# One load for both heads' block of the inverses of the delta-rule scans, issued with the group's features, and two pools opened in the other order

## The chip, the cores and the metric

The kernel runs on one core of a Trainium2 chip, as one launch. The metric is the device time of that launch in microseconds (us). The core has TensorE (PE; PEld is its weight load), VectorE (DVE), ScalarE (ACT), GpSimd (POOL) and SyncE (SP), which here issues the transfers (DMAs).

## The reference

The reference is a trunk of two layers on 256 latent and 256 context tokens of width 2048, in float32. Layer 0 is a bidirectional RWKV-7 mixer with 32 heads of 64, layer 1 is a retention with 8 heads; each stands between an RMSNorm with adaLN and a gated residual add. The change lies in layer 0. Its core, cut to what matters, is this recurrence for each direction and head:

```python
def step(S, inp):
    r_t, w_t, k_t, v_t, kk_t, a_t = inp
    sa = jnp.einsum('bhvk,bhk->bhv', S, kk_t)
    S = S * w_t[:, :, None, :] - sa[..., None] * (kk_t * a_t)[:, :, None, :] + v_t[..., None] * k_t[:, :, None, :]
    return S, jnp.einsum('bhvk,bhk->bhv', S, r_t)
S_c, oc = wkv7_scan(S0, r_c, w_c[d], k_c[d], v_c, kk_c, a_c[d], d == 1)
_, ol = wkv7_scan(S_c, r_l, w_l[d], k_l[d], v_l, kk_l, a_l[d], d == 1)
```

The outputs of both directions are added, normed by head, gated with silu(g) and multiplied by `w_out`.

## The kernel before

**Stages.** Layer 0 runs through `layer0_proj` (the big projections), `layer0_k` (features of the scans from L658 on) and `scans` (L1205); then comes layer 1. The recurrence is not run token by token. Tokens are cut into chunks of 64; inside a chunk the delta rule is a triangular system. Its matrix is inverted by blocks of 32, and the chunk then takes a few matrix products.

**Names.** `layer0_k` writes the features of 16 tiles (two heads each) to `fD` in DRAM, and the 32x32 blocks to invert to `Ld`. `inverse` (L1100) runs for a pair of tiles E on POOL: it loads 128 blocks into invX (L1108), makes 30 steps of a multiply and an add (L1116, L1123), sets the diagonal (L1127), stores the inverses to `Td` (L1131), and after a transposed copy on DVE (L1133) half of them to `T1d` (L1134).

**The scans** take pairs of tiles E = 0, 2, ..., 14, each in four groups q. For a group, `loads` brings the features of both tiles into two of four ft buffers: 512 columns each (L1225, 512 KB; a chunk's matrices), 384 (L1232) and 128 (L1233), and four uv transfers (L1230). `tloads` brings the inverses: at q = 0 two t1 loads (L1261), and for every group eight loads of 32 partitions x 4 x 32 numbers (L1267, 16 KB) into one of two tt buffers, one for each chunk half, block and head. An ft buffer is free again when the products of `outs` (L1420, L1427) have read it, a tt buffer when L1358 has.

In `ahead`, `first` (L1298; needs the ft of 512 columns and t1), ACT's copy L1305, `second` (L1311; needs tt) and ACT's copy L1319 make the blocks' corner in tt; L1286 makes zv. A `step` then takes L1339 (state by features), z on DVE (L1344), L1358 (with tt), uv on ACT (L1364), L1371 and the new state on DVE (L1384). Between these stand the products of the output matrix (`out_chunk`, L1552), whose weights are loaded at L1535 and split into two parts, whi on ACT (L1542) and wlo on POOL (L1543); their other operand yx is split likewise (L1523, L1524). `gpass` stores the gate's part ge to `gT` (L796).

**What sets the order.** Every piece of work is given to a wheel with a time, `W.at(time, function, job, needs, frees)`. The wheel sorts the pieces by time, holds one back while a ring of buffers that it needs is full (and whatever belongs to the same job with it), and writes their instructions in that order; for PE, DVE, ACT and POOL it pins the order (L123, L150). SP's queue is not pinned: there the scheduler of the framework puts the transfers in order by its own timeline. SP issues in order, and a transfer that waits holds those behind it. `open_scans2` (L1182) opens the pools of the scans' second half, in the memory that earlier pools left; the place of a pool decides whose release its first users wait for.

## Time and profile before

| what | value |
|---|---|
| runs: median, lowest, highest of 3 | 2752.47, 2752.12, 2758.63 us |
| profiled execution, its own time | 2755.28 us |
| its span | 2753.5 us |
| busy PE, DVE, ACT, POOL | 2633.9, 1518.4, 1311.2, 746.4 us |
| the scans | about 1000 to 1680 us of the span |
| tt loads (L1267) | 256, of 16 KB, landing 2.3 us after issue (median) |
| ft loads of 512 columns (L1225) | 64, of 512 KB, landing 6.1 us after issue (median) |

One execution is taken by the profiler; starts count from the beginning of its span. In a timeline row stand start, length, engine, line, operation, out<-in, and in brackets the idle time before and what ended it. In a row by window stand the window, its length, the busy time of PE, PEld, DVE, ACT and POOL with their instructions, the granted clock of TensorE (1.00 is full), the share of time in which the 16 DMA engines were busy, and GB/s. SPq is SP's queue, where a row's length is that of the issue, not of the transfer.

### The profile page before, as it was taken

What the parts mean: (1) busy time and instruction counts of PE and PEld (TensorE: products, weight loads), DVE (VectorE), ACT (ScalarE), POOL (GpSimd) and SP (SyncE); (2) the same over time, 40 slices, a digit from 0 to 9 for tenths busy, and PEclk for the clock granted to TensorE, in tenths of its full rate; (3) what the DMA queues carried; (4) which work ended last, traced back from release to release, by engine and by line L of the source; (5) the groups of instructions that cost most, each with busy time, mean ns of one, the idle gap of its engine ahead of it and who ended that gap; (6) DMA issues with size and microseconds to landing.
All of it is one profiled execution on the core that took longest, in us unless ns stands there. A gap on an engine that the chain in (4) does not pass through costs nothing. (4 is left out here: it accounts for less than half of the span.)

```text
span 2753.5 us, 48167 instructions
## 1 busy us (share of the span) xinstructions
PE 2633.9 (96%) x18572; PEld 2137.5 (78%) x18580; DVE 1518.4 (55%) x2629; ACT 1311.2 (48%) x2212; POOL 746.4 (27%) x843
## 2 busy tenths in 40 slices
PE   6999999999998999988999998999999999999998
PEld 5576578777776778867778785888888888899886
DVE  3565853668888822344444456955555644434444
ACT  5243742567777634544444444544445433334443
POOL 0002400000004765665666532300000099600000
PEclk9999999999999999998999999999999999999999
DMA  9868884469899787776767665655555766545654
GB/s 335 311 245 309 287 286 127 138 196 276 259 267 270 226 240 199 198 232 200 213 192 203 165 193 192 227 205 176 171 173 180 257 221 225 196 138 159 202 192 159
DMA packets 543095, 594.70 MB, mean 216 GB/s; under 512 B 118017, under 2 KB 375953, under 8 KB 540049
## 3 DMA queue, kind: packets, MB, share of 16 engines
q1 hardware_dynamic: 542866, 591.62, 68.2%
q8 instruction: 147, 2.41, 0.4%
q14 instruction: 82, 0.67, 0.1%
HBM read 464.11 MB, written 127.40 MB: 215 GB/s over the span
## 5 line engine op out<-in xcount | busy, mean ns | idle before, releaser
L400 DVE TENSOR_TENSOR wlo<-wraw,whi 128x1024 fp32r<-128x1024 f32 (+1 forms) x368 | 462.8, 1259 | 563.3 <-ACT whi L399 557.5
L399 ACT CAST whi<-wraw 128x1024 fp32r<-128x1024 f32 (+1 forms) x368 | 375.4, 1024 | 603.0 <-PE ps_acc L426 177.0
L426 PE MATMUL ps_acc<-whi,xop 128*128 128x512 f32 x1024 | 305.3, 393 | 1.3 <-DVE ev L648 0.8
L1926 PE MATMUL ps_acc<-xop,whi 128*128 128x256 f32 (+1 forms) x1024 | 253.9, 340 | 1.3 <-ACT xop L1677 1.1
L426 PEld LDWEIGHTS ps_acc<-whi,xop 128*128 128x128 f32 x1024 | 192.3, 189 | 45.3 <-issue 2.9
L1552 PE MATMUL ps_b<-yx,whi 128*128 128x512 f32 x512 | 206.9, 441 | 7.6 <-ACT yx L1523 6.4
L1926 PEld LDWEIGHTS ps_acc<-xop,whi 128*128 128x128 f32 x1024 | 176.7, 191 | 24.2 <-ACT xop L1677 1.4
L1826 PEld LDWEIGHTS ps_b<-ax,xop 128*128 128x128 f32 x1536 | 190.8, 188 | 4.9 <-DVE ah L400 0.3
L1826 PE MATMUL ps_b<-ax,xop 128*128 128x256 f32 x1536 | 194.4, 282 | 0.1
L426 PE MATMUL ps_acc<-wlo,xop 128*128 128x512 f32 x512 | 186.7, 392 | 0.0
L1899 POOL TENSOR_TENSOR wga<-wga,cst 128x512 f32<-128x512 f32 x64 | 69.3, 1103 | 415.6 <-DMA wga<-in_ada_w 415.6
L1364 ACT ACTIVATE uv<-ps_p 64x128 f32<-64x128 f32 x256 | 69.7, 272 | 230.4 <-PE ps_p L1358 217.0
L732 PE MATMUL ps_acc<-xop,whi 128*128 128x512 f32 x512 | 177.0, 405 | 2.0 <-DVE ev L648 2.0
L583 PE MATMUL ps_acc<-xop,whi 128*128 128x512 f32 x512 | 161.6, 401 | 14.3 <-ACT xop L399 13.2
L1926 PE MATMUL ps_acc<-xop,wlo 128*128 128x256 f32 (+1 forms) x512 | 171.8, 338 | 1.1 <-DVE wlo L400 1.1
L1384 DVE SCALAR_TENSOR_TENSOR s<-ps_p,ec,qs 64x64 f32<-64x64 f32 x384 | 108.5, 283 | 100.7 <-PE ps_p L1371 89.9
L1876 PE MATMUL ps_acc<-whi,ah 128*128 128x512 f32 x512 | 161.5, 395 | 1.9 <-DVE ah L400 1.9
L426 PE MATMUL ps_c<-whi,xop 128*128 128x512 f32 x512 | 155.4, 390 | 0.0
L1123 POOL TENSOR_TENSOR invX<-invX,invT 128x30 f32<-128x30 f32 (+14 forms) x240 | 134.3, 560 | 15.7
L583 PEld LDWEIGHTS ps_acc<-xop,whi 128*128 128x128 f32 x512 | 95.9, 191 | 53.4 <-ACT xop L399 16.8
L1543 POOL TENSOR_TENSOR wlo<-wraw,whi 128x512 fp32r<-128x512 f32 (+1 forms) x48 | 79.5, 1656 | 203.8 <-ACT whi L1542 186.4
L1116 POOL TENSOR_TENSOR invT<-invX 128x30 f32<-128x30 f32 (+14 forms) x240 | 125.2, 521 | 16.4 <-DMA invX<-Ld 1.1
(300 smaller groups left out, 5588.5 us busy)
## 6 DMA issues: line engine op xcount, KB each, us to landing
wada<-in_ada_w SPq DMA_DIRECT2D x72, 1024.0 KB, 8.5
wraw<-in_rt_w_in SPq DMA_DIRECT2D x64, 1024.0 KB, 5.2
wraw<-in_rk_w_in SPq DMA_DIRECT2D x72, 512.0 KB, 4.8
fD<-it SPq DMA_DIRECT2D x64, 512.0 KB, 4.2
ft<-fD SPq DMA_DIRECT2D x64, 512.0 KB, 6.1
wraw<-in_rt_w_in SPq DMA_DIRECT2D x64, 512.0 KB, 4.6
wraw<-in_rt_w_out SPq DMA_DIRECT2D x32, 1024.0 KB, 5.1
wraw<-in_rk_w_in SPq DMA_DIRECT2D x28, 1024.0 KB, 5.9
```

The costliest lines, as they stand in the source:

```text
L399: self.nc.scalar.copy(hi, src)
L400: (eng or self.nc.vector).tensor_tensor(lo, src, hi.bitcast(F32), ALU.subtract)
L426: nc.tensor.matmul(pt, xop(d)[:, x_, xs], ws[k // 2][w_][:, k % 2, sl], start=(d == 0 and n == 0), stop=(d == nk - 1 and n == 2))
L583: nc.tensor.matmul(acc[i], (hi, lo)[w_][:, kk, 128 * i:128 * i + 128], xs[ds[k]][:, x_, :], start=(k == 0 and n == 0), stop=(k == nk - 1 a ...
L732: nc.tensor.matmul(st["acc"][i], st["s", d // 4][w_][:, d % 4, 128 * i:128 * i + 128], self.kx[d][:, x_, :], start=(d == 0 and m == 0), st ...
L1116: nc.gpsimd.tensor_tensor(tmp[:, 0:j, 0:n], X[:, 0:j, j].unsqueeze(2).broadcast_to([128, j, n]), X[:, j, j + 1:].unsqueeze(1).broadcast_to ...
L1123: nc.gpsimd.tensor_tensor(X[:, 0:j, j + 1:], X[:, 0:j, j + 1:], tmp[:, 0:j, 0:31 - j], ALU.add)
L1384: nc.vector.scalar_tensor_tensor(dst, src, ec, R["qs", d][H, H], ALU.mult, ALU.add)
L1552: nc.tensor.matmul(Q["p", i], Q["s", i // 2][w_][:, k, 128 * (i % 2):128 * (i % 2) + 128], st["yx", e0 + k][:, x_, :], start=(k == 0 and r ...
L1826: nc.tensor.matmul(pt[:, TL * j:TL * j + TL], ht[e][:, w_, 128 * k:128 * k + 128], ax[:, k, x_, :], start=(k == 0 and n == 0), stop=(k == ...
L1876: nc.tensor.matmul(acc[m], y[:, x_, kk, 128 * m:128 * m + 128], ws[w_][:, kk, :], start=(p == 0 and kk == 0 and n == 0), stop=(p == 7 and ...
L1926: nc.tensor.matmul(acc[i][:, 0:nt], w_[:, kk, 128 * i:128 * i + 128], x[:, x_, 0:nt], start=(d == 0 and n == 0), stop=(d == KD - 1 and n = ...
```

## The change

The tiles tt, `Td` and `Ld` get another order of dimensions, in which the two heads' blocks of a chunk lie beside each other. So one transfer of 32 partitions x 8 x 32 numbers (32 KB) takes the place of two of 32 x 4 x 32 (16 KB), four for a group rather than eight; the runs in DRAM stay 32 numbers (128 B). The readers of tt and t1 index accordingly, and ACT's copy L1319 now writes with heads and slots exchanged. `tloads` is no longer a piece of its own at `h0 - 3.0 * Ts`; it stands in the same piece as `loads`, behind it, and so is held by the ft ring too. In `open_scans2` the pool wp1 (whi, wlo) is opened ahead of sp2 (yx and others).

The diff:

```diff
--- before.py
+++ after.py
@@ -665,7 +665,7 @@
 
         self.fD = self.dr.tile([KD, 4, 128, 2, 1024], F32, name="fD")
 
-        self.Ld = self.dr.tile([8, 2, 2, 2, 2, 8, 32, 32], F32, name="Ld")
+        self.Ld = self.dr.tile([8, 2, 2, 8, 2, 2, 32, 32], F32, name="Ld")
         kps = ExitStack()
         kp = kps.enter_context(tc.tile_pool(name="kp", bufs=1, side="right"))
         if True:
@@ -1031,7 +1031,7 @@
                         it, hb = F["it"], 64 * (1 - p)
                         for blk in range(2):
                             r0 = hb + 32 * blk
-                            nc.sync.dma_start(self.Ld[e // 2, blk, p, e % 2, 1 - p if d else p].rearrange("u i t -> i u t"),
+                            nc.sync.dma_start(self.Ld[e // 2, blk, p, :, e % 2, 1 - p if d else p].rearrange("u i t -> i u t"),
                                               it[r0:r0 + 32, :, :, hb + 32 * blk:hb + 32 * blk + 32]
                                               .rearrange("i n h t -> i (n h) t"))
                         nc.sync.dma_start(self.fD[e, :, :, d, 256 * p:256 * p + 256].rearrange("m q r -> q m r"),
@@ -1105,7 +1105,7 @@
 
         def load():
             st["X"] = X = self.ip.tile([128, 32, 32], F32, name="invX", tag="invX")
-            nc.sync.dma_start(X, self.Ld[g].rearrange("b p e x u i t -> (b p e x u) i t"))
+            nc.sync.dma_start(X, self.Ld[g].rearrange("b p u e x i t -> (b p u e x) i t"))
 
         def mul(j):
             def f():
@@ -1128,7 +1128,7 @@
 
         def store():
             X = st["X"]
-            nc.sync.dma_start(self.Td[g].rearrange("b p s n h i t -> (b p s n h) i t"), X)
+            nc.sync.dma_start(self.Td[g].rearrange("b p n u i t -> (b p n u) i t"), X)
             Y = st["tmp"][0:64]
             nc.vector.tensor_copy(Y, X[0:64].rearrange("p j t -> p t j"))
             nc.sync.dma_start(self.T1d[g].rearrange("p u i t -> (p u) i t"), Y)
@@ -1164,7 +1164,7 @@
             self.ft.append(t)
         self.tt = []
         for b in range(2):
-            t = sp.tile([128, 4, 2, 128], F32, name=f"tt{b}", tag=f"tt{b}")
+            t = sp.tile([128, 2, 4, 128], F32, name=f"tt{b}", tag=f"tt{b}")
             nc.gpsimd.memset(t, 0.0)
             self.tt.append(t)
 
@@ -1185,8 +1185,8 @@
         self.x1s, self.s2s = ExitStack(), ExitStack()
         x1p = self.x1s.enter_context(self.tc.tile_pool(name="x1p", bufs=1))
         self.x1 = x1p.tile([128, KD, T], F32, name="x1")
+        self.wp = self.s2s.enter_context(self.tc.tile_pool(name="wp1", bufs=1))
         self.sp2 = self.s2s.enter_context(self.tc.tile_pool(name="sp2", bufs=1))
-        self.wp = self.s2s.enter_context(self.tc.tile_pool(name="wp1", bufs=1))
 
     def chain_psum(self):
 
@@ -1263,9 +1263,8 @@
                     for p in range(2):
                         for blk in range(2):
                             r0 = 64 * (1 - p) + 32 * blk
-                            for h in range(2):
-                                nc.sync.dma_start(tt[r0:r0 + 32, :, h, r0:r0 + 32],
-                                                  self.Td[E // 2, blk, p, :, n, h].rearrange("s i t -> i s t"))
+                            nc.sync.dma_start(tt[r0:r0 + 32, :, :, r0:r0 + 32].rearrange("i h s t -> i (h s) t"),
+                                              self.Td[E // 2, blk, p, n].rearrange("u i t -> i u t"))
                 return f
 
             def ahead(E, q):
@@ -1296,7 +1295,7 @@
                         hb, o = 64 * (1 - p), 64 * slot(e, d, p) + 32 * h
                         n = seq[0][2 * q] // 2
                         nc.tensor.matmul(P["x"][hb + 32:hb + 64, o:o + 32], st[e][q, d]["it"][hb:hb + 32, p, h, hb + 32:hb + 64],
-                                         st[E]["t1"][hb:hb + 32, 8 * slot(e, d, p) + 2 * n + h, :], start=True, stop=True)
+                                         st[E]["t1"][hb:hb + 32, 8 * n + 4 * h + slot(e, d, p), :], start=True, stop=True)
 
                 def cp1():
                     P["xs"] = self.sp.tile([128, 256], F32, name="x21", tag="x21", bufs=1)
@@ -1309,14 +1308,14 @@
                     for e, d, h, p in units:
                         hb, o = 64 * (1 - p), 64 * slot(e, d, p) + 32 * h
                         nc.tensor.matmul(P["y"][hb:hb + 32, o:o + 32], P["xs"][hb + 32:hb + 64, o:o + 32],
-                                         st[E]["tt", q][hb + 32:hb + 64, slot(e, d, p), h, hb + 32:hb + 64], start=True, stop=True)
+                                         st[E]["tt", q][hb + 32:hb + 64, h, slot(e, d, p), hb + 32:hb + 64], start=True, stop=True)
 
                 def cp2():
                     st[E][q, "ready"] = True
                     for p in range(2):
                         hb = 64 * (1 - p)
                         r = slice(hb, hb + 32)
-                        nc.scalar.copy(st[E]["tt", q][r, :, :, hb + 32:hb + 64],
+                        nc.scalar.copy(st[E]["tt", q][r, :, :, hb + 32:hb + 64].rearrange("p h s c -> p s h c"),
                                        P["y"][r, 0:256].rearrange("p (s h c) -> p s h c", h=2, c=32))
 
                 return zv, zvc, first, cp1, second, cp2
@@ -1355,7 +1354,7 @@
                         bank()
                     rhs = R["z"] if s else st[E]["zv", 0][:, k, :]
                     for h in range(2):
-                        nc.tensor.matmul(R["p"][:, 128 + 64 * h:192 + 64 * h], st[E]["tt", q][:, k, h, :],
+                        nc.tensor.matmul(R["p"][:, 128 + 64 * h:192 + 64 * h], st[E]["tt", q][:, h, k, :],
                                          rhs[:, 64 * h:64 * h + 64], start=True, stop=True)
 
                 def uc(d):
@@ -1603,8 +1602,7 @@
                 Ts = (te[E + 2] - te[E]) / 16
                 for q in range(4):
                     h0 = te[E] + 4 * Ts * q
-                    W.at(h0 - LD if E or q else tl + 1.5, loads(E, q), "fl", tuple(("f", FR, (e, q)) for e in (E, E + 1)))
-                    W.at(h0 - 3.0 * Ts if E or q else tl + 1.5, tloads(E, q))
+                    W.at(h0 - LD if E or q else tl + 1.5, (lambda *f: lambda: [g() for g in f])(loads(E, q), tloads(E, q)), "fl", tuple(("f", FR, (e, q)) for e in (E, E + 1)))
                     zv, zvc, first, cp1, second, cp2 = ahead(E, q)
                     j = (E, "i", q)
                     W.at(h0 - 0.9 * Ts, first, j, (("c", 2, (j, 0)),))
@@ -1996,7 +1994,7 @@
                 self.xs = e2.enter_context(tc.tile_pool(name="xs", bufs=1, side="right"))
                 self.layer0_proj(es)
                 e2.close()
-                self.Td = self.dr.tile([8, 2, 2, 4, 4, 2, 32, 32], F32, name="Td")
+                self.Td = self.dr.tile([8, 2, 2, 4, 8, 32, 32], F32, name="Td")
                 self.T1d = self.dr.tile([8, 2, 32, 32, 32], F32, name="T1d")
                 e3 = self.e3 = ExitStack()
                 self.ip = e3.enter_context(tc.tile_pool(name="ip", bufs=1, side="right"))
```

**Order on the engines.** On PE, DVE, ACT and POOL the instructions of the scans stand in the order of before. Three places follow; in each the rows of before stand first.

SP at the head of the pair E = 8, from the store of its inverses on (tt_8770 is the first tt buffer, ft_8764 and ft_8766 the two tiles' features):

```order
L1131 DMA Td<-invX 128x1024
L1134 DMA T1d<-invT 64x1024
L1108 DMA invX<-Ld 128x1024
L1261 DMA t_12749<-T1d 32x32x32 x2
L1267 DMA tt_8770<-Td 32x4x32 x8
L1232 DMA ft_8764<-fD 128x2x384
L1225 DMA ft_8764<-fD 128x2x512
L1230 DMA uv<-vcD 64x2x128
L1225 DMA ft_8766<-fD 128x2x512
L1230 DMA uv<-vcD 64x2x128 x3
L1233 DMA ft_8764<-fD 128x2x128
```

and now:

```order
L1131 DMA Td<-invX 128x1024
L1134 DMA T1d<-invT 64x1024
L1108 DMA invX<-Ld 128x1024
L1261 DMA t_12672<-T1d 32x32x32 x2
L1266 DMA tt_8770<-Td 32x8x32 x4
L1233 DMA ft_8764<-fD 128x2x128
L1232 DMA ft_8764<-fD 128x2x384
L1225 DMA ft_8764<-fD 128x2x512
L1230 DMA uv<-vcD 64x2x128
L1225 DMA ft_8766<-fD 128x2x512
```

Four rows stand where eight stood, still ahead of the features, and the 128-column load (L1233) has moved ahead of the first 512-column one. At E = 6 the same two rows stand ahead of it in both kernels; there the second 512-column load has moved ahead of its tile's two small ones. At E = 14 the load of gb (L2008, now L2006) has moved ahead of the tt loads from behind the features.

SP at the second group of the same pair (tt_8772 is the second tt buffer, ft_8768 and ft_8762 the other two ft):

```order
L1535 DMA wraw<-in_rk_w_out 128x4x512
L1267 DMA tt_8772<-Td 32x4x32 x6
L1232 DMA ft_8768<-fD 128x2x384
L1225 DMA ft_8768<-fD 128x2x512
L1230 DMA uv<-vcD 64x2x128
```

and now:

```order
L1534 DMA wraw<-in_rk_w_out 128x4x512
L1266 DMA tt_8772<-Td 32x8x32 x4
L1233 DMA ft_8768<-fD 128x2x128
L1232 DMA ft_8768<-fD 128x2x384
L1225 DMA ft_8768<-fD 128x2x512
```

Before, two of the eight trailed behind the features; now all four stand ahead of them.

ACT at the first split of the output matrix, with the semaphores that a row waits for (DMAHW are transfers; in the first piece DMAHW1 and in the second DMAHW3 counts the last store to gT):

```order
L1364 ACTIVATE uv<-ps_p_11104 64x128 [waits DMAHW5_49,DMAHW4_49,PE_49]
L1364 ACTIVATE uv<-ps_p_11104 64x128
L1542 CAST whi<-wraw 128x512 [waits DMAHW7_49,DMAHW1_49]
L1523 CAST yx<-y_10117 128x512 [waits Pool_49]
L1349 ACTIVATE qs<-s_8776,ec 128x128 [waits DVE_49]
```

and now:

```order
L1363 ACTIVATE uv<-ps_p_11064 64x128 [waits DMAHW1_49,DMAHW0_49,PE_49]
L1363 ACTIVATE uv<-ps_p_11064 64x128
L1541 CAST whi<-wraw 128x512 [waits Pool_49]
L1522 CAST yx<-y_10093 128x512 [waits DMAHW3_49]
L1348 ACTIVATE qs<-s_8776,ec 128x128 [waits DVE_49]
```

The order is the same; the wait for the store to gT has moved from whi to the yx behind it.

## The prediction

> **What bounds the kernel now.** I read the page first, then PE's waits in the scans (1000 to 1690 us), the timelines of PE and SP around the longest of them, and the stretches by window. On the page:
>
> ```profile
> span 2753.5 us, 48167 instructions
> PE 2633.9 (96%) x18572; PEld 2137.5 (78%) x18580; DVE 1518.4 (55%) x2629; ACT 1311.2 (48%) x2212; POOL 746.4 (27%) x843
> ```
>
> TensorE is busy for 96% of the span, so time can come only from its idle time or from work that runs at a lower clock. Its longest waits in the scans (total, times, longest):
>
> ```profile
> PE ps_c L1298 <- DMA ft<-fD: 17.0, 10, 3.0
> PE ps_p L1358 <- DVE z L1344: 7.8, 4, 2.9
> PE ps_b L1552 <- ACT yx L1523: 6.4, 1, 6.4
> ```
>
> The first is the one that the change bears on: `first` (L1298) waits for the features. PE's timeline shows where (start, length, last in brackets the idle time before); it is at the head of the pairs E = 6, 8, 10 and 14:
>
> ```profile
> 1261.91 0.63 PE L1298 MATMUL ps_c<-t,ft 32*32 32x32 f32 x16 [2.32 <-DMA ft<-fD]
> 1265.52 0.64 PE L1298 MATMUL ps_c<-t,ft 32*32 32x32 f32 x16 [2.98 <-DMA ft<-fD]
> 1266.08 1.97 PE L1286 MATMUL ps_c<-uv,ft 64*64 64x64 f32 x32
> 1300.30 1.15 PE L1286 MATMUL ps_c<-uv,ft 64*64 64x64 f32 x32
> 1335.50 0.44 PE L1298 MATMUL ps_c<-t,ft 32*32 32x32 f32 x16 [1.16 <-DMA ft<-fD]
> 1337.78 0.64 PE L1298 MATMUL ps_c<-t,ft 32*32 32x32 f32 x16 [1.84 <-DMA ft<-fD]
> 1410.20 0.44 PE L1298 MATMUL ps_c<-t,ft 32*32 32x32 f32 x16 [0.75 <-DMA ft<-fD]
> 1412.41 0.64 PE L1298 MATMUL ps_c<-t,ft 32*32 32x32 f32 x16 [1.77 <-DMA ft<-fD]
> 1572.08 0.64 PE L1298 MATMUL ps_c<-t,ft 32*32 32x32 f32 x16 [2.68 <-DMA ft<-fD]
> 1575.18 0.64 PE L1298 MATMUL ps_c<-t,ft 32*32 32x32 f32 x16 [2.46 <-DMA ft<-fD]
> ```
>
> Idle: 5.30 at E = 6, 3.00 at E = 8, 2.52 at E = 10, 5.14 at E = 14, together 16.0 of the 17.0. Such a stall costs more than its idle time: the 32 products of L1286 take 1.97 us right behind one, 1.15 where PE had hardly waited (1300.30). The windows behind the four show why (length, PE busy, PEld, DVE, ACT, POOL, granted clock, DMA share, GB/s):
>
> ```profile
> 1261.50:1275.10 13.60, 10.22 (x150) 9.00 (x151) 0.00 (x0) 3.69 (x9) 5.42 (x9) 0.50 0.28 80
> 1336.60:1343.30 6.70, 5.52 (x57) 4.95 (x58) 0.00 (x0) 1.89 (x6) 0.00 (x0) 0.50 0.95 284
> 1411.70:1418.40 6.70, 5.99 (x58) 4.96 (x58) 0.00 (x0) 2.36 (x6) 0.00 (x0) 0.50 0.81 242
> 1572.10:1578.80 6.70, 4.24 (x67) 3.73 (x68) 0.00 (x0) 1.31 (x3) 0.00 (x0) 0.50 0.97 264
> ```
>
> The clock is 0.50 in all four. Half of the busy time is the loss: 5.1, 2.8, 3.0 and 2.1 us. With the idle time the four stalls cost 29 us.
>
> Why the features are late is in SP's timeline before E = 6, and in one row of E = 14:
>
> ```profile
> 1248.66 6.25 SPq L1267 DMA_DIRECT2D tt<-Td  x8
> 1255.01 0.53 SPq L1233 DMA_DIRECT2D ft<-fD  x1
> 1255.64 0.56 SPq L1232 DMA_DIRECT2D ft<-fD  x1
> 1256.29 0.56 SPq L1225 DMA_DIRECT2D ft<-fD  x1
> 1256.94 1.25 SPq L1230 DMA_DIRECT2D uv<-vcD  x2
> 1258.29 0.56 SPq L1232 DMA_DIRECT2D ft<-fD  x1
> 1258.89 0.60 SPq L1233 DMA_DIRECT2D ft<-fD  x1
> 1259.59 0.56 SPq L1225 DMA_DIRECT2D ft<-fD  x1
> ...
> 1560.27 5.55 SPq L1267 DMA_DIRECT2D tt<-Td  x8
> ```
>
> SP issues back to back, and the eight small transfers stand 6.25 and 5.55 us in front of the features; E = 8 and 10 I take to be like E = 14. The DMA engines are not the limit meanwhile; while SP is still at these issues their share is 0.20 (the figure before last), and 0.87 once the features are out:
>
> ```profile
> 1253.50:1256.30 2.80, 2.63 (x19) 2.14 (x19) 1.39 (x5) 1.44 (x5) 2.19 (x5) 1.00 0.20 32
> 1256.30:1259.60 3.30, 2.78 (x18) 1.96 (x16) 2.33 (x8) 0.54 (x2) 2.40 (x7) 1.00 0.87 246
> ```
>
> So a feature load that is issued earlier should land about as much earlier: at E = 6 the two 512-column loads were issued at 1256.29 and 1259.59, and PE went on at 1261.91 and 1265.52, 5.6 and 5.9 us later.
>
> **The change, part by part.** *Four transfers rather than eight.* 128 issues go, bytes and runs (128 B) stay. What one of double size costs to issue is not in the trace; these are the nearest rows (ns, least/median/most):
>
> ```profile
> L1267 SPq DMA_DIRECT2D tt<-Td x256: 302/430/1934, 1007.2 to 1615.5; - x128
> L1261 SPq DMA_DIRECT2D t<-T1d x16: 318/554/2005, 998.5 to 1559.6; - x16
> ```
>
> A t load has 1024 runs of 128 B, a tt load 128, and their medians are 554 and 430 ns. So 256 runs should cost hardly more than 430. But eight times 0.43 is 3.4, not 6.25: at each pair's head one or two of the eight take up to 1.9 us. If these long ones stay (they may stand for the runs queued ahead of them), four issues save 4 x 0.43 = 1.7 us; if they go in proportion, half, 2.8 to 3.1. I take 2.0, nearer the low end, with the gap between two issues in it. The Trainium skill, "DMA: Bandwidth & Descriptors", Rules for kernel authors, says to coalesce small transfers, since below 64 KB one pays mostly overhead; by that the price hangs on the count and the saving would be half, the upper end. No run here shows a 32 KB transfer.
>
> *The order on SP.* By the words of the change the transfers stand behind the features; by SP's order they do not. The queue is not pinned, and all four still stand ahead of the group's features. At E = 8, 10 and 14 the 128-column load (L1233) now precedes the first 512-column one, a row of 1255.64 - 1255.01 = 0.63 us later; at E = 6 the second 512-column load comes ahead of the two small ones (1259.59 - 1258.29 = 1.3 us earlier). At E = 14 the gb load now stands ahead of the tt loads, and waits for a POOL memset; I put that at 0 to 1 us, 0.5 taken, from one or two issues of SP.
>
> E = 6: first load 2.0 earlier, so the first wait shrinks from 2.32 to 0.3; second 3.3 earlier, so PE goes on at 1262.2 and not at 1265.52: -3.3. E = 8 and 10: 2.0 - 0.63 = -1.4 each. E = 14: -0.9. Sum **-7.0**, between -5 (the 1.7) and -11 (half).
>
> *The clock.* Left idle: 2.0 at E = 6, 1.6 at E = 8, 1.1 at E = 10, 4.2 at E = 14. Halved clock follows 2.52 us of idle (E = 10 before); it does not follow the short wait before 1300.30. I take it to vanish at E = 10 and 8 (3.0 + 2.8), and to stay at E = 6 and 14: **-5.8**, between 0 and -13.0. The Trainium skill, "TensorE: Matmul & The Clock Gate", Part 1, has the clock halve after an idle window of about 3.4 us; by that E = 10 should have kept its clock with 2.52 us of idle in two pieces. The trace speaks against it there.
>
> *The pools.* These rows are of ACT and POOL at the 6.4 us wait:
>
> ```profile
> 1198.67 0.62 ACT L1542 CAST whi<-wraw 128x512 fp32r<-128x512 f32 x1 [7.38 <-DMA gT<-ge]
> 1199.19 0.61 ACT L1523 CAST yx<-y 128x512 fp32r<-128x512 f32 x1
> 1199.36 1.27 POOL L1543 TENSOR_TENSOR wlo<-wraw,whi 128x512 fp32r<-128x512 f32 x1 [14.19 <-ACT whi L1542]
> 1201.20 1.27 POOL L1524 TENSOR_TENSOR yx<-y,yx 128x512 fp32r<-128x512 f32 x1
> ```
>
> The wait for the store of gT moves from whi to the yx right behind it on ACT. PE needs both, so it still starts when that store has landed: 0.5 us gained. POOL gains more: its wlo no longer stands behind the store, and its yx can run at about 1199.3, not 1201.20. POOL then works nearly without a pause to the end of the inverse for E = 6, from which SP's sequence there starts. So -1.9 at most, 0 if POOL waits for PE in between: I take **-1.5**; PE's own 0.5 lies inside it, since E = 6 is where PE next waits.
>
> Do these gains last? POOL's next inverse cannot go on until PE has passed the stall, since its wlo waits for ACT, which waits for PE:
>
> ```profile
> 1269.29 1.27 POOL L1543 TENSOR_TENSOR wlo<-wraw,whi 128x512 fp32r<-128x512 f32 x1 [10.11 <-ACT whi L1542]
> ```
>
> So POOL moves up with PE, and the next pair's blocks with it. What PE gains inside a pair behind that point is lost again at the wait for z (second row of the waits), which hangs on POOL.
>
> *At nothing:* the ACT copy into tt, which now steps over a strided side:
>
> ```profile
> L1319 ACT COPY tt<-ps_c x64: 362/363/367, 1016.0 to 1633.7; 32x256 f32<-32x256 f32 x64
> ```
>
> No wait for it is among PE's longest, and L1552's products stand between it and its reader. A doubling would be 64 x 0.36 = 23 us on ACT, which is idle for half the span; on PE I put it at 0 to 1. The store to Ld has runs as long as before. Layer 1's start has a few instructions in another order, with no wait behind them that I can see.
>
> Sum: -7.0 - 5.8 - 1.5 = -14.3. The profiled execution is 2755.28 us (span 2753.5), 2.8 above the median of the runs, so the forecast is 2741.0 for its like and 2752.47 - 14.3 = 2738 for the median.
>
> **Rivals.**
> *More.* The long issues go in proportion and the clock holds at E = 6 too. At E = 6 -4.4, at 8 -2.2, at 10 -2.5, at 14 -2.2, together -11.3; clock -10.9; POOL -1.9: 24 us, 2728. For it: the DMA engines stood at 0.20. Against: the 1.9 us rows. If the clock held at E = 14 too, 2.1 more, 2726; the 0.50 behind 2.52 us of idle is against that. The window of 3.4 us in the Trainium skill, "TensorE: Matmul & The Clock Gate", Part 1, would have it so, with idle pieces of some 2 us each.
>
> *No change.* Shortened stalls still halve the clock: 1.1 to 2.0 us of idle may suffice, since E = 10 needed only 2.52. Then -7.0, and part of that goes to the wait for z, 7.8 us of which hang on POOL and not on SP: -3 to -7, 2747.
>
> *Slower.* The issue of a transfer goes by its size, so four cost what eight did. Then the heads gain nothing and lose 0.63 at E = 8, 10 and 14, +1.9, less 1.3 at E = 6. Inside the pairs, where before six tt rows and one feature row stood ahead of the first 512-column load (3.1 us by their medians), four at 0.86 and two feature rows now take 4.6: 1.5 later. There the slack is small, PE waits at six more places of the ten for 1.0 us in all (17.0 - 16.0), so I count some 0.8 at each of eight groups, +6, and with the clock halved behind two or three of them (2.8 each), +7: 2766. It decides from about 0.7 us for an issue. The t row speaks against it: eight times the runs in 554 ns.
>
> **How the numbers follow.** Forecast 0.48, more 0.17, no change 0.25, slower 0.10. A measurement of this kernel tells about 0.3% (8 us) from no change. The forecast has some 0.06 below that bound, so faster 0.58, same 0.31, slower 0.11. The range reaches from the larger gain (2725) over no change to a little above before (2756), and leaves out the slower case and the far end of the larger one.
>
> **What would show it.** Right: four tt issues of 0.4 to 0.5 us, and at most two long ones, ahead of the features; L1298's wait falls from 17.0 to about 9; L1286 at 1.15 us and a clock of 1.00 behind E = 8 and 10. Wrong: tt issues above 0.7 us; feature loads that are issued earlier and land when they did; a clock of 0.50 behind all four heads; or a wait for z that grows by what L1298's loses.

## The result and the profile after

The changed kernel takes 2742.14 us (median of 4 runs, 2738.39 to 2742.83), the kernel before 2755.55 us (4 runs beside it, 2752.12 to 2760.10). The ratio is 0.9947, its 95% interval 0.9935 to 0.9960: 13.4 us less in the medians. Forecast were 14.3 us less.

The page's head after, then PE's waits in the scans (total, times, longest):

```profile
span 2740.6 us, 48026 instructions
PE 2630.5 (96%) x18572; PEld 2133.8 (78%) x18580; DVE 1517.3 (55%) x2629; ACT 1311.4 (48%) x2212; POOL 742.6 (27%) x843
```

```profile
PE ps_p L1357 <- DVE z L1343: 7.7, 4, 2.9
PE ps_c L1297 <- DMA ft<-fD: 6.5, 8, 1.6
PE ps_b L1551 <- ACT yx L1522: 6.1, 1, 6.1
PE ps_b L786 <- ACT whi L776: 2.5, 2, 1.9
```

The wait for the features (L1298, now L1297) has fallen from 17.0 to 6.5 us, 10.5 less; those for z and yx stand as before. PE's timeline at the same four heads (the third row is of E = 8, without any wait):

```profile
1260.62 0.44 PE L1297 MATMUL ps_c<-t,ft 32*32 32x32 f32 x16 [1.52 <-DMA ft<-fD]
1260.99 1.15 PE L1285 MATMUL ps_c<-uv,ft 64*64 64x64 f32 x32
1328.06 0.94 PE L1297 MATMUL ps_c<-t,ft 32*32 32x32 f32 x32
1397.72 0.44 PE L1297 MATMUL ps_c<-t,ft 32*32 32x32 f32 x16 [0.52 <-DMA ft<-fD]
1555.31 0.44 PE L1297 MATMUL ps_c<-t,ft 32*32 32x32 f32 x16 [0.19 <-DMA ft<-fD]
1557.36 0.44 PE L1297 MATMUL ps_c<-t,ft 32*32 32x32 f32 x16 [1.61 <-DMA ft<-fD]
```

3.8 us are left of 16.0 there. SP's timeline at the head of E = 6, and its rows at E = 8 and E = 14:

```profile
1245.48 0.98 SPq L1261 DMA_DIRECT2D t<-T1d  x2
1246.56 3.21 SPq L1266 DMA_DIRECT2D tt<-Td  x4
1249.87 0.53 SPq L1233 DMA_DIRECT2D ft<-fD  x1
1250.49 1.53 SPq L1232 DMA_DIRECT2D ft<-fD  x1
1252.12 0.56 SPq L1225 DMA_DIRECT2D ft<-fD  x1
...
1316.19 2.80 SPq L1266 DMA_DIRECT2D tt<-Td  x4
...
1545.37 2.07 SPq L1266 DMA_DIRECT2D tt<-Td  x4
1547.54 1.69 SPq L1233 DMA_DIRECT2D ft<-fD  x1
```

The tt loads take 3.21 us where they took 6.25, 2.07 where they took 5.55. At E = 6 and 14 a long issue has passed on to a feature load (L1232 with 1.53 us, L1233 with 1.69). The price of an issue did not change with its size (ns, least/median/most):

```profile
L1266 SPq DMA_DIRECT2D tt<-Td x128: 302/444/1733, 1008.5 to 1595.8; - x128
```

Last the windows around the heads of E = 6, 8, 10 and 14 (columns as in the prediction; the third figure from the right is the granted clock):

```profile
1262.10:1268.90 6.80, 6.80 (x86) 5.88 (x86) 0.00 (x0) 2.96 (x7) 5.20 (x8) 0.52 0.15 26
1315.00:1345.00 30.00, 29.46 (x391) 24.99 (x391) 13.49 (x41) 14.42 (x39) 17.07 (x27) 1.00 0.81 225
1385.00:1412.00 27.00, 26.42 (x343) 22.65 (x343) 11.61 (x35) 12.95 (x35) 15.23 (x24) 1.00 0.80 223
1559.00:1562.50 3.50, 3.50 (x15) 2.56 (x11) 0.15 (x1) 1.66 (x4) 0.00 (x0) 0.54 0.33 115
```

Behind E = 8 and 10 the clock is full; behind E = 6 and 14 it is halved for about half as long as before.

Where the time went, from the starts of the same products in both traces: before, 510.73 us lie between the end of the wait for yx (1199.86) and the start of layer 1's first L1926 behind its opening (1710.59). Now they are 492.64 (1201.12 to 1693.76), 18.1 less. The spans differ by 12.9 only. 1.3 us were lost ahead of that stretch (PE's waits in L786 for whi and wlo, at the scans' opening, grew from 1.4 + 0.9 to 2.5 + 1.7 + 0.7 us), and 3.9 behind it, in layer 1. There ACT waited longer for a store of zs, in the second row (after) than in the first (before), and PE behind it:

```profile
2307.11 0.69 ACT L1851 COPY zs<-ps_c 128x256 f32<-128x256 f32 x2 [7.66 <-DMA zT<-zs]
```

```profile
2292.62 0.71 ACT L1849 COPY zs<-ps_c 128x256 f32<-128x256 f32 x2 [9.77 <-DMA zT<-zs]
```

No other kernel with four tt loads below shows a loss of that size there, so I take it for this execution's own.

Two more profiles of the kernel before, told of below, have 505.9 (1203.60 to 1709.53) and 504.9 us (1199.45 to 1704.33) between the same two points. Against them the changed kernel has 12 to 13 us less there, so some 5 of the 18.1 belong to the first profile of before alone.

### The profile page after: what moved, and what is told of

The parts are those of the page before. It is cut to its first block, busy times and chain, and to the rows that moved or that the text cites. A ratio compares the mean times of both kernels' runs of the same rounds, so it can differ in the third digit from the quotient of the medians.

```text
span 2740.6 us, 48026 instructions
## 1 busy us (share of the span) xinstructions
PE 2630.5 (96%) x18572; PEld 2133.8 (78%) x18580; DVE 1517.3 (55%) x2629; ACT 1311.4 (48%) x2212; POOL 742.6 (27%) x843
## 4 chain that ended last, share of the span: by engine, by line
PE 42%; DMA 5%; POOL 4%; DVE 2%; issue 1%; ACT 1%; SPq 0%; DVEq 0%; POOLq 0%; ACTq 0%
PE ps_acc L1924 9%; PE ps_acc L426 6%; PE ps_c L426 6%; PE ps_b L1551 5%; PE ps_acc L1874 5%; PE ps_b L1824 4%; DMA ft<-fD 2%; POOL wga L1897 2%; DMA wga<-in_ada_w 1%; POOL gb L1898 1%; PE ps_p L1370 1%; PE ps_p L1357 1%; PE ps_c L1285 1%; PE ps_p L1338 1%; PE ps_b L1786 1%
## 5 line engine op out<-in xcount | busy, mean ns | idle before, releaser
L399 ACT CAST whi<-wraw 128x1024 fp32r<-128x1024 f32 (+1 forms) x368 | 375.5, 1024 | 599.6 <-PE ps_acc L426 177.6
L1897 POOL TENSOR_TENSOR wga<-wga,cst 128x512 f32<-128x512 f32 x64 | 75.9, 1206 | 421.0 <-DMA wga<-in_ada_w 421.0
L583 PE MATMUL ps_acc<-xop,whi 128*128 128x512 f32 x512 | 161.3, 401 | 15.3 <-ACT xop L399 12.6
L1542 POOL TENSOR_TENSOR wlo<-wraw,whi 128x512 fp32r<-128x512 f32 (+1 forms) x48 | 79.5, 1657 | 180.7 <-ACT whi L1541 165.1
```

The source lines that it names most:

```text
L399: self.nc.scalar.copy(hi, src)
L583: nc.tensor.matmul(acc[i], (hi, lo)[w_][:, kk, 128 * i:128 * i + 128], xs[ds[k]][:, x_, :], start=(k == 0 and n == 0), stop=(k == nk - 1 a ...
L1897: nc.gpsimd.tensor_tensor(w[:, k, :], w[:, k, :], self.cst[:, 2 * x + k, 6:7].broadcast_to([128, 512]), ALU.mult)
```

## The experiments

The theory: what counts is how long SP issues ahead of the features; fewer issues bring them earlier, and the stall's half clock with it. The rivals: the pools carry the gain; or the DMA engines or the bytes set the landing; or the clock is no price that an avoided stall saves. Ratios are to runs of the kernel before on the same chip; "of before" means its median of about 2754 us.

**Which part carries it.** Four loads alone: the changed kernel with tloads at its own place and the pools as before, as a diff to the changed kernel:

```diff
-        self.wp = self.s2s.enter_context(self.tc.tile_pool(name="wp1", bufs=1))
         self.sp2 = self.s2s.enter_context(self.tc.tile_pool(name="sp2", bufs=1))
+        self.wp = self.s2s.enter_context(self.tc.tile_pool(name="wp1", bufs=1))
...
-                    W.at(h0 - LD if E or q else tl + 1.5, (lambda *f: lambda: [g() for g in f])(loads(E, q), tloads(E, q)), "fl", tuple(("f", FR, (e, q)) for e in (E, E + 1)))
+                    W.at(h0 - LD if E or q else tl + 1.5, loads(E, q), "fl", tuple(("f", FR, (e, q)) for e in (E, E + 1)))
+                    W.at(h0 - 3.0 * Ts if E or q else tl + 1.5, tloads(E, q))
```

> The changed kernel with the pools opened as before and the tt loads as a piece of their own again; four loads of 32 KB stay. Theory (what counts is the issue time of the tt loads on SP): tt loads at 0.44 us, four of them in 2 to 3.2 us at the heads of the pairs, L1298's wait about 7 us rather than 17, and the time 9 to 13 us under before, most of the change's 13. Rival (the pools carry the gain, since POOL and with it the chain of stores and loads at E = 6 comes earlier): no more than 5 us under before.

Measured: 0.9957 (0.9942 to 0.9972), 2740.22 us against 2753.64, and L1297's wait is 8.6 us. SP's order at the heads is that of the changed kernel. Its four loads at E = 6 took 5.27 us, with two long issues among them, more than the 2 to 3.2 that were expected; at E = 8, 10 and 14 they took 2.8 to 3.5. So this part alone has the gain, within what can be told.

The pools alone:

```diff
-        self.sp2 = self.s2s.enter_context(self.tc.tile_pool(name="sp2", bufs=1))
         self.wp = self.s2s.enter_context(self.tc.tile_pool(name="wp1", bufs=1))
+        self.sp2 = self.s2s.enter_context(self.tc.tile_pool(name="sp2", bufs=1))
```

> The kernel before with only the two pools opened in the other order. Theory (issue time): the wait for the store of gT moves from whi to yx, PE's wait there stays at about 6 us, POOL is about 2 us earlier at the end of the inverse for E = 6, and the time falls by 1 to 3 us, with L1298's wait still about 17. Rival (the pools carry the gain): 8 us or more under before.

Measured: 0.9984 (0.9972 to 0.9996), 1 to 8 us less. L1298 waits 15.3 us, yx 4.4. That fits the theory's 1 to 3, and excludes the rival's 8 but barely. The 2 us by which POOL was to be earlier are not seen: the store of the inverses for E = 6 (L1131) is issued 38.3 us after the wait for yx ends (1198.11 to 1236.39), in the three profiles of before 37.7 to 38.5 us after it. What the pools add to the four loads is not told apart: 0.9957 and 0.9947 overlap.

The place alone, with eight loads:

```diff
-                    W.at(h0 - LD if E or q else tl + 1.5, loads(E, q), "fl", tuple(("f", FR, (e, q)) for e in (E, E + 1)))
-                    W.at(h0 - 3.0 * Ts if E or q else tl + 1.5, tloads(E, q))
+                    W.at(h0 - LD if E or q else tl + 1.5, (lambda *f: lambda: [g() for g in f])(loads(E, q), tloads(E, q)), "fl", tuple(("f", FR, (e, q)) for e in (E, E + 1)))
```

> The kernel before with only the place of tloads changed (in one piece with the features, behind them); eight loads of 16 KB, pools as before. In SP's order seven of the eight now stand behind the features at E = 6, and all eight ahead of them at E = 8, 10 and 14, as before. Theory (issue time ahead of the features): L1298's wait at E = 6 falls from 5.3 to under 2, the others stay (2 to 5 us each), and the time is 3 to 8 us under before. Rival (the place is worth nothing, or the loads that come late cost as much): within 2 us of before.

Measured: 0.9999 (0.9988 to 1.0010). The expectation failed: the wait of L1298 at E = 6 was 3.53 + 2.83, as long as before, though the first 512-column load was issued 3.2 us after the first t load (1249.28 to 1252.45) and not 8.6 (1247.64 to 1256.29). In that execution PE reached the head 4.6 us after the first t load was issued (1253.85), before 12.0 us after it (1259.59): SP's sequence started that much later relative to PE, which took away what the features had gained behind it. A part of this is that POOL waited 2.35 us for whi (L1542) ahead of the end of the inverse; the rest is open. In the time the place alone is worth nothing.

**Issues or bytes.** The kernel before with each tt load cut in two:

```diff
-                                nc.sync.dma_start(tt[r0:r0 + 32, :, h, r0:r0 + 32],
-                                                  self.Td[E // 2, blk, p, :, n, h].rearrange("s i t -> i s t"))
+                                for u in range(0, 4, 2):
+                                    nc.sync.dma_start(tt[r0:r0 + 32, u:u + 2, h, r0:r0 + 32],
+                                                      self.Td[E // 2, blk, p, u:u + 2, n, h].rearrange("s i t -> i s t"))
```

> The kernel before with every tt load cut in two, so sixteen of 8 KB for a group, bytes and runs the same. Theory (a price for each issue, not for its bytes): an issue still takes 0.43 us in the median, the sixteen take 8 to 12 us at the heads of the pairs, the features come 2 to 4 us later there, and the time is 10 to 25 us above before. Rival (a price by bytes, or the DMA engines bound the landing): an issue takes about half as long, the features land when they did, the time is within 4 us of before.

Measured: 1.0186 (1.0168 to 1.0204), 51 us more, and the two rows of it:

```profile
L1268 SPq DMA_DIRECT2D tt<-Td x512: 302/425/3184, 1006.1 to 1657.4; - x171
```

```profile
PE ps_c L1299 <- DMA ft<-fD: 48.0, 24, 8.6
```

The median issue takes 425 ns with 8 KB, as 430 with 16 and 444 with 32: the price is that of an issue. The rival on bytes falls. The time rose by more than twice the most that I had expected: 24 waits rather than 10, since groups inside the pairs, whose features had come just in time, now wait too; the four heads have some 24 of the 48.0 us, where before they had 16.0 of 17.0. At the heads SP's order is no longer that of before: at E = 6 fourteen of the sixteen stand ahead of the features, in 8.1 us, at E = 8 only ten, in 4.8. 256 issues more cost 0.20 us each at the end, 128 fewer won 0.09 each (11.8 us of the four loads alone).

**Where the long issues come from.** The changed kernel with T1d stored transposed, so that the two t loads ahead of tt read long runs:

```diff
-            nc.sync.dma_start(self.T1d[g].rearrange("p u i t -> (p u) i t"), Y)
+            for p in range(2):
+                nc.sync.dma_start(self.T1d[g, p].rearrange("i u t -> u i t"), Y[32 * p:32 * p + 32])
...
-                            nc.sync.dma_start(t1[hb:hb + 32], self.T1d[E // 2, p].rearrange("u i t -> i u t"))
+                            nc.sync.dma_start(t1[hb:hb + 32], self.T1d[E // 2, p])
```

> The changed kernel with T1d stored transposed (two stores of 32 partitions with runs of 128 B), so that a t1 load reads 4 KB in one run on each partition. Theory (the long issues of 1.6 to 1.9 us come from the 2048 short runs of the two t1 loads ahead of them): the tt issues at the heads are all 0.3 to 0.5 us, four in 1.8 us rather than 2.1 to 3.2, the features come about 1 us earlier there, and the time is 1 to 5 us under the changed kernel's. Rival (the long issues belong to the tt loads or to the whole burst, or the stores now take the time): long tt issues stay and the time is within 2 us of the changed kernel's or above it.

Measured: 0.9935 (0.9923 to 0.9947). SP's rows at the heads of E = 6, 8 and 10:

```profile
1247.16 1.85 SPq L1267 DMA_DIRECT2D tt<-Td  x4
...
1317.32 1.95 SPq L1267 DMA_DIRECT2D tt<-Td  x4
...
1386.97 1.79 SPq L1267 DMA_DIRECT2D tt<-Td  x4
```

All are short now, four in 1.8 to 1.95 us. So the long ones came from the t loads' short runs, paid by whoever was issued next. L1298's wait is 5.8, 0.7 less than in the changed kernel: at E = 6 and 10 the first feature load (L1233, here L1234) now waits 1.9 and 2.0 us for the release of its buffer by `outs` (L1427) instead. By its ratio it is not told apart from the changed kernel.

The changed kernel with the tt loads really behind the features, which its words say and its order does not:

```diff
                                               self.Td[E // 2, blk, p, n].rearrange("u i t -> i u t"))
+                            if E:
+                                tc.add_manual_dep(nc.cur_bb.bb.instructions[-1], st["ft"], mybir.DependencyInfo(
+                                    mybir.DependencyClass.NoSync, mybir.DependencyReason.DATA), reason="line")
```

> The changed kernel with the four tt loads held behind the group's features in SP's order (from the second pair on), which the changed kernel's words say but its order does not. Theory (issue time ahead of the features): the features come 2 to 3 us earlier at the heads, L1298's wait falls from 6.5 to under 3, the half clock behind E = 6 and 14 goes, and the time is 3 to 8 us under the changed kernel's, 16 to 21 under before. Rival (the tt loads then come too late for the products L1311, or the wait for z takes what is gained): within 3 us of the changed kernel, with a wait of L1311 for tt or a longer wait for z in place of L1298's.

Measured: 0.9947 (0.9932 to 0.9963), as the changed kernel, and L1300 waits 7.1: the theory's 3 to 8 us did not come. SP at E = 8:

```profile
1322.14 0.94 SPq L1261 DMA_DIRECT2D t<-T1d  x2
1323.17 1.90 SPq L1233 DMA_DIRECT2D ft<-fD  x1
1325.16 0.56 SPq L1232 DMA_DIRECT2D ft<-fD  x1
1325.81 0.56 SPq L1225 DMA_DIRECT2D ft<-fD  x1
1326.42 0.60 SPq L1230 DMA_DIRECT2D uv<-vcD  x1
1327.08 1.36 SPq L1225 DMA_DIRECT2D ft<-fD  x1
```

With the tt loads gone from there the long issues fall on the features (1.90 and 1.36 us, where 0.56 is usual). The first 512-column load follows the end of the t loads by 2.7 us rather than 4.2 (there it is issued at 1320.31, and the t loads end at 1316.09), and PE has not gained by it: here it reached the head 9.6 us after the first t load was issued (1322.14 to 1331.78), in the changed kernel 13.3 us after it (1314.73 to 1328.06). As with the place alone, what the features gain behind the t loads is lost in a later start of SP's sequence relative to PE. Why it starts later is not shown. The rival's new waits, for tt or z, did not come either (z 7.8). The two edits above together:

> The changed kernel with both edits: T1d stored so that a t1 load reads one run of 4 KB on each partition, and the tt loads held behind the features. Theory (what stands ahead of the features on SP): two short issues alone stand between the load of invX and the features, L1298's wait falls under 4 us, and the time is 1 to 4 us under that with the t1 edit alone (0.9935 of before). Rival (what is left at the heads comes from the landing of the stores to Td and from the wait for z, not from SP's issues): the same as the t1 edit alone within 2 us.

Measured: 0.9940 (0.9922 to 0.9958), 2739.49 us, and L1301's wait is 2.7 us, as the theory had it; the time is not below that of the t edit alone. So less than 3 us are left of 17.0 in this wait, and the last 3 to 4 of them bought nothing that can be measured: the wait for z (7.8) and that for yx (5.6) are now the larger ones.

**What the half clock is worth.** The kernel before with products without use where PE sat idle:

```diff
-                    for e, d, h, p in units:
+                    for u, (e, d, h, p) in enumerate(units):
+                        if q == 0 and E in (6, 8, 10, 14) and u in (0, 8):
+                            for _ in range(4 + u // 8):
+                                nc.tensor.matmul(P["x"][:, 256:384], self.ident, self.ident, start=True, stop=True)
```

> The kernel before with nine products without use (128x128 by 128x128) added at the heads of E = 6, 8, 10 and 14, four ahead of the first half of L1298 and five between the halves, where TensorE sat idle for 2.5 to 5.3 us. Theory (the idle time halves the clock, and that costs 5.1 + 2.8 + 3.0 + 2.1 us more than the idle itself): the clock behind E = 8 and 10 stays at 1.00 and mostly behind the others, and the time falls by 4 to 10 us though work is added. Rival (the half clock hangs on something else than idle time, or is short of an effect on the end): the 0.50 stretches stay, the time is the same or up to 6 us longer.

Measured: 1.0004 (0.9994 to 1.0015). At E = 8 and 10 it did what was meant (E = 8 in PE's timeline, and the windows at both); at E = 6 and 14 some idle time and some half clock were left (6.7 and 3.3 us at 0.50):

```profile
1340.08 1.06 PE L1298 MATMUL ps_c<-c_ident 128*128 128x128 f32 x8
1341.06 0.44 PE L1301 MATMUL ps_c<-t,ft 32*32 32x32 f32 x16
1341.43 1.38 PE L1298 MATMUL ps_c<-c_ident 128*128 128x128 f32 x10
1342.97 0.44 PE L1301 MATMUL ps_c<-t,ft 32*32 32x32 f32 x16 [0.15 <-DMA ft<-fD]
```

```profile
1340.00:1350.00 10.00, 9.85 (x178) 8.46 (x177) 1.07 (x3) 4.51 (x10) 2.34 (x2) 1.00 0.77 232
1412.50:1422.00 9.50, 9.50 (x178) 8.22 (x177) 1.07 (x3) 4.23 (x10) 2.07 (x1) 1.00 0.66 199
```

The idle time is filled and the clock stays at 1.00 there, and yet the time does not fall. The same at E = 8 and 10 alone, where the products hardly delay anything:

```diff
-                        if q == 0 and E in (6, 8, 10, 14) and u in (0, 8):
+                        if q == 0 and E in (8, 10) and u in (0, 8):
```

> The kernel before with the nine products at the heads of E = 8 and 10 alone, where they cover the idle time without outlasting it. Theory (the half clock behind a head is worth its share in the end): the 0.50 stretches behind E = 8 and 10 are gone, and the time falls by 3 to 6 us (2.8 + 3.0). Rival (what TensorE wins there is lost again, at the next wait for z or by half clocks that fall elsewhere): within 2 us of before.

Measured: 0.9998 (0.9985 to 1.0011): between 4 us less and 3 more. The 5.8 us that I had put on these two heads are excluded. In its trace the clock is 1.00 behind both heads. From the first product of L1298 in the last group of E = 6 to that at E = 12 PE takes 169.4 us (1316.07 to 1485.48), 173.2, 172.1 and 172.1 in the three profiles of the kernel before: some 3 us were won there. About as much was lost again between, behind a wait for z (first row) after which the clock is 0.50 (second row); in the profile that the forecast was made on it is 1.00 from 1430 to 1471 us, around the same wait, of 1.70 us there:

```profile
1458.22 0.66 PE L1361 MATMUL ps_p<-z,tt 128*128 128x64 f32 x4 [1.72 <-DVE z L1347]
```

```profile
1459.90:1466.70 6.80, 6.50 (x76) 5.61 (x77) 1.51 (x6) 1.75 (x5) 0.00 (x0) 0.50 1.06 279
```

Half of the 6.50 us busy is 3.2 us. This is what the rival said, seen in one execution; the run with products at all four heads has such a stretch at the same place (1469.3 to 1476.0). And the first set of products on top of the changed kernel, by the same edit:

> The changed kernel with the same nine products at the heads of E = 6, 8, 10 and 14. Theory: little idle time is left there (1.5, 0, 0.5 and 1.6 us), so the products cost about what they cover and a little clock is won behind E = 6 and 14: within 4 us of the changed kernel's time. Rival (the clock is worth more than the idle): 4 us or more under the changed kernel.

Measured: 0.9946 (0.9934 to 0.9958), the changed kernel's own ratio: nothing won, as the theory had it. In its profile the mean clock from 1215 to 1640 us is 0.99, in the changed kernel's 0.97. But nine products take 2.4 us at a head (1.06 + 1.38 above), 9.8 at four, and only 3.8 us of idle time was left there, so this run can't tell what the clock is worth.

How steady the half clock is can be seen when the kernel before is profiled again, twice and without an edit:

> The kernel before, unchanged, for a second profile of it. Theory (the half clock behind the heads is a fixed price of their idle time): the waits of L1298 at E = 6, 8, 10 and 14 are within 1 us of the first profile's 5.3, 3.0, 2.5 and 5.1, and the 0.50 stretches stand behind the same four heads, 13.6, 6.7, 6.7 and 6.7 us long. Rival (where the half clock falls changes from execution to execution): like waits, but a 0.50 stretch missing behind one or two of the heads, or standing behind other waits.

> The kernel before, unchanged, for a third profile of it; what each theory expects is as for the second: the same four stretches of half clock behind the heads, or others.

Measured: 2753.77 and 2749.72 us. L1298 waits 17.6 and 16.8 us between 1215 and 1640 us, as in the first profile (17.0). But the half clock stands elsewhere. In the second profile, at the heads of E = 8 and 10 (idle 0.51 + 2.25 and 1.23 + 2.21 us):

```profile
1337.84 0.44 PE L1298 MATMUL ps_c<-t,ft 32*32 32x32 f32 x16 [0.51 <-DMA ft<-fD]
1340.53 0.44 PE L1298 MATMUL ps_c<-t,ft 32*32 32x32 f32 x16 [2.25 <-DMA ft<-fD]
```

```profile
1338.00:1348.00 10.00, 7.75 (x161) 6.55 (x157) 0.45 (x2) 5.01 (x11) 2.78 (x3) 1.00 0.79 230
1411.50:1424.50 13.00, 11.31 (x131) 9.40 (x133) 0.00 (x0) 4.21 (x9) 4.08 (x5) 0.50 0.50 146
1575.00:1578.00 3.00, 3.00 (x30) 2.59 (x26) 0.00 (x0) 0.95 (x3) 0.00 (x0) 0.50 0.77 253
```

Behind 2.76 us of idle at E = 8 the clock stays at 1.00, behind 3.44 at E = 10 it is 0.50 for 13 us, where the first profile had 6.7 behind both. In the third profile it is 0.50 for 6.7 us behind 1.81 us of idle at E = 8, for 10.1 behind 3.17 at E = 10 and for 3.4 behind 3.00 at E = 14. So behind a stall of 1.8 to 3.5 us the clock is halved for no time at all, or for 3, 7, 10 or 13 us, and which it is changes from execution to execution of one kernel. The Trainium skill, "TensorE: Matmul & The Clock Gate", Part 1, says that the window by which the gate judges is free-running, so that the point at which the clock changes depends on where in it the work falls. The three profiles agree with that: the stretches last about one to four times 3.41 us and begin whole multiples of it apart (in the prediction's windows 1261.5, 1336.6, 1411.7 and 1572.1 us, which is 22, 22 and 47 steps).

This does not yet explain why the filled idle time won so little. By the prediction's measure (half of the busy time) the half clock behind E = 8 and 10 together cost 5.8, 5.7 and 8.4 us in the three profiles: it moved between the two heads, but the sum was there each time.

From 1215 to 1640 us the mean clock is 0.94, 0.96 and 0.96 in the three profiles of before, and 0.97 in that of the changed kernel:

```profile
1215.00:1640.00 425.00, 392.28 (x4800) 334.40 (x4804) 197.89 (x574) 189.54 (x510) 238.69 (x341) 0.94 0.71 200
```

```profile
1215.00:1640.00 425.00, 404.80 (x4943) 342.65 (x4946) 208.67 (x606) 197.56 (x529) 245.26 (x346) 0.97 0.71 207
```

The first profile, on which the forecast was made, had the most half clock of the three, and it is also the one that took 5 us longer over the scans' second half (510.7 against 505.9 and 504.9 us, above). So it can't be said that the clock counts for nothing.

## Why the prediction was right, and where its steps failed

The sum was right (-14.3 forecast, -13.4 measured), and so was what it rests on: the number of tt loads on SP. The four loads alone and the sixteen bracket it. How fewer issues reach the time is shown only in part: the two runs that took tt loads out of their place ahead of the features won nothing. The terms came out thus:

- **Issues of the tt loads, forecast 2.0 us saved at each head: right but for E = 14.** The tt rows shrank by more, 3.0, 2.8, 2.5 and 3.5 us at E = 6, 8, 10 and 14 (6.25 to 3.21, 5.62 to 2.80, 6.41 to 3.96, 5.55 to 2.07). But the long issues did not go with the count: at these heads six issues of over 1 us stand before and seven after, and two of them now fall on feature loads. So the low end was right, and the upper end, half, did not arrive at the features. The rule on small transfers in the Trainium skill, "DMA: Bandwidth & Descriptors", Rules for kernel authors, by which one pays mostly overhead under 64 KB, agrees in that 32 KB in one issue cost 444 ns in the median and 16 KB 430. What arrived is this, in us after the issue of the first t load; behind the arrow stands the changed kernel, in brackets the second and third profile of before:

| head | first 512-column load is issued | PE reaches L1298 |
| --- | --- | --- |
| E = 6 | 8.65 -> 6.64 (9.51, 8.54) | 11.95 -> 13.18 (10.38, 9.49) |
| E = 8 | 7.36 -> 5.58 (7.28, 7.36) | 10.97 -> 13.33 (12.40, 13.00) |
| E = 10 | 8.15 -> 6.29 (8.08, 7.85) | 13.11 -> 12.75 (12.27, 12.23) |
| E = 14 | 7.31 -> 7.23 (7.34, 7.62) | 10.16 -> 12.37 (12.38, 11.91) |

- **Idle time at the heads, forecast -7.0: too small, but not by the issues.** It fell by 12.2 (16.0 to 3.8), L1298's wait as a whole by 10.5, since inside the pairs PE now waits for 2.7 us and not 1.0. The features' earlier issue gives 3.3 (the second 512-column load at E = 6, 11.95 to 8.64, as forecast) + 1.8 + 1.9 + 0.1 = 7.1, the forecast. The rest is in the last column: PE reaches three of the heads 1.2 to 2.4 us later after the t loads, a distance that the sum had taken as fixed ("POOL moves up with PE"). At E = 8 and 14 the other two profiles of before stand near the changed kernel, so that it may be the first profile's own; at E = 6 the distance is longer than in all three. What moved it is not shown.
- **The clock, forecast -5.8: the step that failed.** It fell as forecast in this one profile (full behind E = 8 and 10, half behind 6 and 14), but as a price that an avoided stall saves it was wrong: the idle time filled at just those heads won 4 us at most, though half of the busy time at 0.50 there is 5.7 to 8.4 us in the three profiles of before. Some 3 us of it are seen to be lost again at a wait for z in one execution; whether that is the rule stays open. What part of the 13.4 us is clock stays open too: the mean clock of the stretch rose, by 0.01 to 0.03, and a rise of 0.01 over 425 us is 4 us.
- **The pools, forecast -1.5.** The wait for gT's store moved to yx as the order says, and POOL's yx stands at 1201.15 in a trace whose PE is 1.3 us later there. Alone they gave 1 to 8 us, on top of the four loads nothing that can be told.
- **At nothing:** L1318 takes 362 to 366 ns for 362 to 367, with no wait for it. The gb load at E = 14 delayed the tt loads by 1.1 us at most (the t loads end at 1544.17, tt begins at 1545.37), where 0 to 1 was allowed for and 0.5 taken. With it and the long issue on L1233, E = 14 kept only 0.1 us of the 0.9 that the sum gave it.
- **Not foreseen:** the waits of L786 at the opening (2.5 + 1.7 + 0.7 us where they were 1.4 + 0.9, or 2.0 + 1.1 and 2.3 + 1.0 in the other two profiles of before), and inside the pairs the new waits named above.

Two errors met: the idle term was 3 to 5 us too small, the clock term too large by an amount that the runs do not fix. That the sum came within 1 us is luck. The slower rival falls with the 444 ns; "no change" was right in that shortened stalls may still halve the clock (1.52 us of idle at E = 6, then 6.8 us at 0.52).

## What to carry to other kernels

On a queue that issues in order, count the issues that stand ahead of the transfer that someone waits for: here each cost 0.43 to 0.44 us whether it carried 8, 16 or 32 KB, and the transfers of many short runs before them were paid for by the next in line. Read SP's real order, not the place in the code: "behind the features" stood ahead of them, and where they did stand behind, it won nothing, since SP's sequence then started later relative to PE. So count from the event that starts the sequence, and look whether that event moves. And don't book the half clock behind a short stall as a fixed price: profile the same kernel again first.

## What the runs showed of the hardware

- An issue on SP takes 425 to 444 ns in the median from 8 to 32 KB (128-byte runs); behind two loads of 1024 such runs each, at most heads one or two issues take 1 to 3 us, whichever transfer they belong to. With long runs in those loads the tt issues behind them take about 0.45 us; with the tt loads moved away as well, single feature issues of 1.25 to 1.48 us are left at three heads.
- After 1.8 to 3.5 us of idle time at a head TensorE's clock was halved for 0, 3, 7, 10 or 13 us in executions of one and the same kernel; the stretches lie on a grid of 3.41 us.
